# A decoder layer in split single precision: quarter-weight sums and residual operations bound behind given VectorE instructions, at other places, residual tiles in pairs

## The chip, the cores and the metric

One core of one Trainium2 chip runs one program with one launch. The metric is the device time of one execution in microseconds, as the median of several executions. The kernel before takes 1776.06 us (median of 3 executions, 1775.77 to 1781.95).

## The reference, cut to what matters

Sequence of 2048 tokens, width 1024, hidden width 4096, all in float32.

```python
mod = (silu(c) @ w_ada + b_ada)[:, None, :]
sh1, sc1, g1, sh2, sc2, g2 = split(mod, 6)
h = x * (1.0 + sc1) + sh1
gate_b, gate_c, v_conv, v_pool = split(h @ w_in, [512, 1024, 1536])
y_conv = gate_b * short_conv(gate_c * v_conv, conv_w)
y_pool = multiscale_pool(v_pool, w_pool, pool_scale)
mix = concatenate([y_conv, y_pool]) @ w_out
x = layer_norm(ALPHA * x + (1.0 + g1) * mix, ln1_g, ln1_b)
h = x * (1.0 + sc2) + sh2
f = square(relu(h @ w_mlp_in)) @ w_mlp_out
out = layer_norm(ALPHA * x + (1.0 + g2) * f, ln2_g, ln2_b)
```

The change touches two things that this leaves implicit. One is the term `ALPHA * x` of the last line, where x is the first normalisation's output with its scale and shift: the "residual". The other is the weight `w_mlp_out`, of which sums of blocks are formed for a fast product.

## The kernel before, in words

**Split products.** Every matrix product is made of three passes: an operand is cast to a rounded high part on ScalarE (line 84), VectorE subtracts to get the low part (line 85), and TensorE multiplies high by high, high by low and low by high (lines 89 to 91), 128 by 128 weights against 512 columns.

**Seven products in place of eight.** All large products use a Winograd form: of a 2 by 2 partition of both operands, seven block products are formed from sums of blocks, and the results are put together in PSUM banks and by copies and adds. The sums of weight blocks are made by the kernel itself (`sum_blocks`, lines 949 to 960): for each half, four loads by the sync queue, four VectorE operations of 128 by 512, and four stores to DRAM by the GpSimd queue. The operations are all recorded at line 94, the helper `tt`.

**Two blocks of 1024 tokens.** For b = 0 and b = 1 the kernel runs the input projection, the output projection with the first normalisation, the "up" product with relu and square (8 groups of 512 hidden channels, `up`), and the "down" product with the last normalisation (`down`). Up results go to DRAM (`usum`) and are loaded again as operands of down.

**Quarters.** In block 1 three of the seven products of down (FINE) are themselves done by seven products of quarter size (`fine_product`, line 1155 for the matmuls). For these the up groups save quarters of their results (`save_quarters`, `uquart`), and quarter sums of the weights are needed (`quarter_sums`, `wquart`): twelve sums, taken in turn from the list `quarters`. Before the change four of them are written into block 0's down product, at its steps 6, 8, 10 and 12, with tiles "c"; four into block 1's input projection, two each for its groups 1 and 2, with tiles "c"; and four into block 1's up product, after groups 2, 4, 5 and 7 (QUARTER_SUMS), with tiles "o". All are needed before block 1's fine products.

**The residual.** The first normalisation stores its unscaled rows in `nsave`, eight tiles of 128 tokens in each block. Two VectorE operations a tile (`rest_of`, lines 983 and 984) apply the scale and shift rows and ALPHA, and the result is stored in `rsave`, from where the end of down loads it. In block 0 this is done during down (`residual`, two tiles at each of four steps). In block 1 tiles 0 to 3 are done in up groups 1, 3, 5 and 6 (REST): after the second of the seven products the group loads two broadcast rows and the tile (`rest_loads`), and after the fourth `rest_of` is written. Tiles 4 to 7 are done during down (`rest_late`): two at step 0, one at step 2, one at step 4.

**The down product's steps.** Block 0 has 14 steps, each of four operands that are loaded, cast and split one step ahead (`down_operands`); block 1 has 8 and the fine products. Some steps end tile by tile (`by_tile`), so that a finished tile's normalisation can start early (`first_row`, `second_row`, `last`).

**What sets the order.** The text of the kernel gives each instruction's place in a priority order. A planner with a model of durations lays out each engine's stream: an instruction whose inputs and buffers are free in the model may be taken ahead of others that stand before it in the text. On the chip every engine's stream, the queue of transfers on SyncE and that on GpSimd included, is then executed strictly in that order. `tc.issue_after(x)` puts the instructions of its block on x's engine behind x in that order; transfers on other engines are not bound by it. Tiles come from rings by name: "o" has 10 buffers, "c" 2, "r" 5, "w" 6, "h" 28; PSUM has 8 banks. A load into a tile waits until the last user of the buffer is done, a store's landing included.

Of the kernel before, what the change touches and what calls it, by code (L numbers as in the profile page):

```python
# [14 lines left out]
D = 1024  # L15
# [13 lines left out]
HALO = 16  # L29
Q = H // 2  # L30
HALF_SUMS = (1, 2, 3, 3, 3, 3, 3, 0)
QUARTER_SUMS = (0, 0, 1, 0, 1, 1, 0, 1)
EARLY, WARM = 4, 14
WW = T + HALO

# [8 lines left out]
def tile_hybrid_layer(ctx: ExitStack, tc: tile.TileContext, opening, xT, x, wada, vec, win0, win,  # L44
# [20 lines left out]
    def t_o(w=T, dt=F32):  # L65
        return mk(big, [P, w], dt, "o", 10)
# [21 lines left out]
    def mm3(ps, whi, wlo, xhi, xlo, first, last, goes_on=False):  # L88
        nc.tensor.matmul(ps, whi, xhi, start=first, stop=False, skip_group_check=goes_on)  # L89
        nc.tensor.matmul(ps, whi, xlo, start=False, stop=False, skip_group_check=goes_on)  # L90
        nc.tensor.matmul(ps, wlo, xhi, start=False, stop=last, skip_group_check=goes_on)  # L91

    def tt(out_, a, b_, op):
        return nc.vector.tensor_tensor(out_, a, b_, op=op)  # L94


    vecs = cp.tile([P, 104], F32, name="vecs")
# [524 lines left out]
    def in_proj_1(X, W, first_w):  # L622
# [83 lines left out]
        for j in range(1, NG):  # L706
            last = j == NG - 1
            next(groups[j])
            if not last:
                quarter_sums(t_c)  # L710
                next(groups[j])
                quarter_sums(t_c)
            next(groups[j - 1], None)
            if last:
                next(groups[j])
            next(groups[j])
        next(groups[-1], None)
        return ops

# [229 lines left out]
    def sum_blocks(src, dst, tiles=t_o, which=halves):  # L949
        for p in which:  # L950
            a, b_ = tiles(T), tiles(T)
            b22, b12, b11, b21 = a[:, :H], a[:, H:], b_[:, :H], b_[:, H:]
            for i, r in ((3, b22), (1, b12), (0, b11), (2, b21)):
                nc.sync.dma_start(r, src[i][:, p])
            tt(b22, b22, b12, ALU.subtract)
            tt(b12, b12, b11, ALU.subtract)
            tt(b11, b22, b11, ALU.add)
            tt(b21, b21, b11, ALU.subtract)
            for i, r in ((2, b22), (0, b12), (1, b11), (3, b21)):
                nc.gpsimd.dma_start(dst[i][:, p], r)  # L960

    FINE = {0: 2, 1: 0, 5: 1}
    QUARTERED = {1: 0, 7: 1, 0: 2}
    REST = {1: 0, 3: 1, 5: 2, 6: 3}
    UQ = {"11": 0, "12": 1, "22": 2, "s1": 3, "s2": 4, "s3": 5, "s4": 6}

    def save_quarters(r, n, g):
# [18 lines left out]

    quarters = [(n, hf, p) for n in (2, 0, 1) for hf in range(2) for p in halves]

    def quarter_sums(tiles):
        n, hf, p = quarters.pop(0)  # L990
        sum_blocks([w2q[n, i, hf] for i in range(4)], wquart[n, hf], tiles, [p])

    def sum_out(g, tiles):
        sum_blocks([gout[i % 2, i // 2 * 2 + g] for i in range(4)], wosum[g], tiles)
# [1 line left out]
    def up(g, B, fine):  # L996
        X, Y, Z = {}, {}, {}
        order = (0, 1, 5, 4, 6, 7, 3) if g else (0, 1, 7, 4, 5, 6, 3)
        product = seven(summed_weights(w1[g], w1sum[g], order) if g < 2 else block_weights(w1[g]), B)
        ps = [slice(p * H, p * H + H) for p in range(2)]  # L1000

        def keep(banks, tile=t_o):
            r = tile()
            for p in range(2):
                nc.scalar.copy(r[:, ps[p]], banks[p])
            return r

        def add(r, banks):
            for p in range(2):
                tt(r[:, ps[p]], r[:, ps[p]], banks[p], ALU.add)  # L1010

        def join(r, banks):
            add(r, banks)
            nc.scalar.activation(r, r, AF.Relu)
            nc.scalar.activation(r, r, AF.Square)

        def save(r, i):
            if fine and i in QUARTERED and (i or g > 1):
                save_quarters(r, QUARTERED[i], g)
            else:  # L1020
                nc.gpsimd.dma_start(usum[g, i], r)

        def rest_loads():
            if fine and g in REST:
                r, ag, ab = t_o(D), row(t_o(D), rows[0]), row(t_o(D), rows[1])
                nc.sync.dma_start(r, nsave[REST[g]])
                return r, ag, ab

        product(0, X, True)
# [12 lines left out]
        product(2, X, False)  # L1042
        c12 = keep(X)
        if g == 0:
            add(c12, Y)
            join(c12, Z)
            yield
        else:
            product(3, Z, True)
            c22 = keep(Z)  # L1050
        if loaded:
            rest_of(REST[g], *loaded)
        product(4, X, False)
        join(c22, X)
        save(c22, 3)
        if g == 0:
            yield
        else:
            product(5, Z, False)
            join(c12, Z)  # L1060
        s1 = t_o()
        tt(s1, c12, c22, ALU.add)
        tt(c12, c11, c12, ALU.subtract)
        tt(c11, s1, c11, ALU.subtract)
        for i, r in ((4, s1), (6, c12), (5, c11)):
# [53 lines left out]
    def down(b, F, g2, close):  # L1119
# [159 lines left out]
            table[3] = Y, True, third_row  # L1279
        base = 5  # L1280
        by_tile = (3, 4, 6) if b else (4, 5, 6)
        for t in range(8):
            F.append(t_o(D))
        ready = operands(0)
        later = rest_late() if b else residual()
        todo = [(k, m) for k in FINE for m in range(7)]
        for n, (i, hf) in enumerate(steps):
            ops, _ = ready
# [145 lines left out]
    def mlp(b, B, back, g2):  # L1434
# [14 lines left out]
        for g in range(NC):  # L1449
            for _ in ups[g]:  # L1450
                pass
            if b and g in (3, 4):
                c11 = t_o()
                nc.sync.dma_start(c11, usum[g - 3, 0])
                save_quarters(c11, QUARTERED[0], g - 3)
# [79 lines left out]
```

## Time and profile before

| what | value |
|---|---|
| median of 3 executions | 1776.06 us (1775.77 to 1781.95) |
| the profiled execution's own time | 1773.37 us |
| its span, first to last instruction | 1771.6 us |
| TensorE busy, share of the span | 1734.4 us, 98% |
| VectorE busy | 1391.9 us, 79% |
| ScalarE busy | 888.8 us, 50% |
| GpSimd (mostly issuing stores) | 272.0 us, 15% |
| mean granted TensorE clock | 0.989 |
| moved by DMA | 504.64 MB, mean 285 GB/s |

How to read the profile: the page gives one profiled execution. A group row names line, engine, operation, out<-in tiles, shape and count, then busy time and mean duration, then how long the engine was idle just before and what ended that. The timeline gives one instruction a row: start, duration, engine, line, operation, tiles, and in brackets the idle time before it and its releaser. A row of a stretch gives for each engine the busy time and the count, then the granted clock of TensorE, the share of the 16 DMA engines' time, and GB/s. Matmuls of 512 columns follow each other about every 0.23 us, though each is shown as 0.39 us long, because they overlap.

### The profile page before, as it was taken

Reading aid. Unit: us, or ns where it says so; the run is one execution under the profiler, and the core shown is the slowest. Engines: PE = TensorE matmul, PEld = TensorE weight load, DVE = VectorE, ACT = ScalarE, POOL = GpSimd, SP = SyncE. Lnnn points to the kernel's source line nnn. Section 1 sums busy time; section 2 is a strip of 40 time slices with the busy share of each in tenths; the row PEclk is TensorE's granted clock in tenths of the full one; section 3 lists DMA queues with packets and bytes.
Section 4 is the critical chain, followed back from the end, with each engine's and each line's share of the span. In section 5 each row is a group of like instructions: output and inputs, shape, how many; then the busy total and the mean of one; then the engine's idle time right before and its main releaser. Section 6 shows DMA issues by size and latency. Waiting matters only on the chain.

```text
span 1771.6 us, 22926 instructions
## 1 busy us (share of the span) xinstructions
PE 1734.4 (98%) x8142; PEld 1452.7 (82%) x8142; DVE 1391.9 (79%) x1840; ACT 888.8 (50%) x1206; POOL 272.0 (15%) x483
## 2 busy tenths in 40 slices
PE   9999999999999999988999999999999999999998
PEld 8888888888888788866888888878887788999887
DVE  8897788777677776768886789687667677888997
ACT  5323467545444655333673344764444454877451
POOL 0222220123222001111000100103222212000020
PEclk9999999999999999989999999999999999999999
DMA  9999876688887999997872366657677779998871
GB/s 387 344 327 343 301 270 236 263 323 327 325 326 292 344 404 365 353 369 275 282 258 96 107 220 220 215 212 258 214 260 266 263 261 354 418 382 304 294 275 60
DMA packets 157715, 504.64 MB, mean 285 GB/s; under 512 B 18832, under 2 KB 19616, under 8 KB 157600
## 3 DMA queue, kind: packets, MB, share of 16 engines
q1 hardware_dynamic: 108000, 329.61, 51.2%
q0 software_dynamic: 49600, 173.58, 25.6%
q8 instruction: 63, 1.03, 0.2%
q14 instruction: 52, 0.43, 0.1%
HBM read 345.29 MB, written 157.82 MB: 284 GB/s over the span
## 4 chain that ended last, share of the span: by engine, by line
PE 65%; issue 13%; DMA 11%; DVE 8%; POOL 2%; ACT 1%; SPq 0%; DVEq 0%; POOLq 0%; ACTq 0%
PE ps L89 18%; PE ps L90 18%; PE ps L91 18%; PE ps L1155 6%; DVE o L94 3%; PE ps L409 2%; DVE h L85 2%; DMA usum<-c 2%; DMA o<-in_xT 2%; DMA r<-in_w 2%; DVE w L85 1%; DMA c<-in_wada 1%; DMA o<-in_w2q 1%; PE ps L762 1%; DMA r<-uquart 1%
## 5 line engine op out<-in xcount | busy, mean ns | idle before, releaser
L89 PE MATMUL ps<-h,w 128*128 128x512 f32 x1312 | 512.5, 391 | 6.6 <-DVE o L94 6.3
L90 PE MATMUL ps<-h,w 128*128 128x512 f32 x1312 | 512.2, 391 | 1.6 <-DVE h L85 1.6
L91 PE MATMUL ps<-h,w 128*128 128x512 f32 x1312 | 511.8, 390 | 0.4 <-DVE w L85 0.4
L89 PE MATMUL ps<-h,h 128*128 128x512 f32 (+1 forms) x936 | 365.8, 391 | 11.3 <-ACT o L1216 7.3
L90 PE MATMUL ps<-h,h 128*128 128x512 f32 (+1 forms) x936 | 365.9, 391 | 6.0 <-DVE h L85 6.0
L91 PE MATMUL ps<-h,h 128*128 128x512 f32 (+1 forms) x936 | 365.3, 390 | 0.0
L84 ACT CAST h<-r 128x1024 fp32r<-128x1024 f32 (+1 forms) x202 | 205.7, 1022 | 258.7 <-PE ps L90 68.2
L89 PEld LDWEIGHTS ps<-h,w 128*128 128x128 f32 x1312 | 247.2, 189 | 60.4 <-DVE o L94 8.1
L90 PEld LDWEIGHTS ps<-h,w 128*128 128x128 f32 x1312 | 247.2, 188 | 53.3 <-DVE h L85 2.3
L91 PEld LDWEIGHTS ps<-h,w 128*128 128x128 f32 x1312 | 247.3, 188 | 52.7 <-DVE w L85 0.8
L85 DVE TENSOR_TENSOR h<-r,h 128x1024 fp32r<-128x1024 f32 (+1 forms) x202 | 239.0, 1188 | 45.2 <-ACT h L84 44.6
L84 ACT CAST w<-r 128x1024 fp32r<-128x1024 f32 x156 | 164.3, 1054 | 208.8 <-PE ps L90 202.6
L85 DVE TENSOR_TENSOR w<-r,w 128x1024 fp32r<-128x1024 f32 x156 | 190.5, 1221 | 64.4 <-ACT w L84 63.3
L89 PEld LDWEIGHTS ps<-h,h 128*128 128x128 f32 x936 | 177.6, 190 | 49.9 <-ACT o L1216 7.7
L90 PEld LDWEIGHTS ps<-h,h 128*128 128x128 f32 x936 | 177.3, 189 | 43.5 <-DVE h L85 7.6
L91 PEld LDWEIGHTS ps<-h,h 128*128 128x128 f32 x936 | 177.5, 190 | 36.2
L85 DVE TENSOR_TENSOR h<-w,h 128x1024 fp32r<-128x1024 f32 x130 | 160.7, 1236 | 12.7 <-ACT h L84 12.5
L84 ACT CAST h<-w 128x1024 fp32r<-128x1024 f32 x130 | 136.6, 1051 | 9.3 <-DMA w<-in_w 3.4
L94 DVE TENSOR_TENSOR o<-o,o 128x512 f32<-128x512 f32 (+2 forms) x158 | 122.8, 782 | 5.5 <-DMA o<-hsave 2.4
L1155 PE MATMUL ps<-h,h 128*128 128x256 f32 x1008 | 122.9, 285 | 2.1 <-ACT o L1165 2.1
L1155 PEld LDWEIGHTS ps<-h,h 128*128 128x128 f32 x1008 | 122.6, 194 | 2.4 <-ACT o L1165 2.3
L94 DVE TENSOR_TENSOR o<-o,ps 128x512 f32<-128x512 f32 (+1 forms) x150 | 95.8, 650 | 27.8 <-PE ps L91 23.1
(174 smaller groups left out, 1542.9 us busy)
## 6 DMA issues: line engine op xcount, KB each, us to landing
r<-usum SPq DMA_DIRECT2D x88, 512.0 KB, 5.9
w<-w2sum SPq DMA_DIRECT2D x64, 512.0 KB, 6.2
r<-in_w SPq DMA_DIRECT2D x60, 512.0 KB, 6.4
usum<-o POOLq DMA_DIRECT2D x56, 512.0 KB, 4.6
r<-uquart SPq DMA_DIRECT2D x42, 512.0 KB, 8.0
o<-in_w SPq DMA_DIRECT2D x72, 256.0 KB, 5.7
usum<-c POOLq DMA_DIRECT2D x34, 512.0 KB, 5.2
w2sum<-o POOLq DMA_DIRECT2D x64, 256.0 KB, 5.8
```

The source lines that it names most:

```text
L84: high = nc.scalar.copy(hi, src)
L85: return high.ins, nc.vector.tensor_tensor(lo, src, hi.bitcast(F32), op=ALU.subtract).ins
L89: nc.tensor.matmul(ps, whi, xhi, start=first, stop=False, skip_group_check=goes_on)
L90: nc.tensor.matmul(ps, whi, xlo, start=False, stop=False, skip_group_check=goes_on)
L91: nc.tensor.matmul(ps, wlo, xhi, start=False, stop=last, skip_group_check=goes_on)
L94: return nc.vector.tensor_tensor(out_, a, b_, op=op)
L409: nc.tensor.matmul(ps[m, h], wt[:, w : w + P], A[k][p // 2][:, hs], start=k == 0 and p == 0, stop=k == KD - 1 and p == 2)
L762: nc.tensor.transpose(ps[:, t * P : t * P + P], R[4 * h + t][:, k * P : k * P + P], ident)
L1155: nc.tensor.matmul(ps, a[:, us], w[:, gs], start=not begun, stop=hf == 1 and g == 3 and a is ul, skip_group_check=True)
```

## The change

The four edits:

1. `tt` remembers its last instruction in `recent`. `quarter_sums` takes an instruction, and its VectorE operations are bound behind that.
2. The places of the twelve quarter sums: five in block 0's down product (steps 2, 3, 6, 7, 10, each behind the last split of the next step's operands), four in block 1's input projection (behind the last `tt` at two places of groups 1 and 2, the second place now at the end of the turn), three in block 1's up product (after groups 1, 3 and 5). The tiles of the gate vector's loads (`ada` at steps 0 and 1) come from "o" in place of "c". The quarters of groups 0 and 1 that are loaded again (`save_quarters`) are bound too, after groups 3 and 5 in place of 3 and 4.
3. Block 1's residual tiles 0 to 5 are done in pairs in up groups 2, 4 and 6. Two rows and two tiles are loaded at the same place as before, and the operations are written at the end of the group, bound behind its last `tt`.
4. Residual tiles 6 and 7 are both done at step 0 of block 1's down product, bound behind the last split of the next step's operands. Their rows come from "o" tiles that are taken before the eight result tiles.

```diff
-QUARTER_SUMS = (0, 0, 1, 0, 1, 1, 0, 1)
+QUARTER_SUMS = (0, 1, 0, 1, 0, 1, 0, 0)
...
+    recent = [None]
+
     def tt(out_, a, b_, op):
-        return nc.vector.tensor_tensor(out_, a, b_, op=op)
+        done = nc.vector.tensor_tensor(out_, a, b_, op=op)
+        recent[0] = done.ins
+        return done
...
             if not last:
-                quarter_sums(t_c)
+                quarter_sums(t_c, recent[0])
                 next(groups[j])
-                quarter_sums(t_c)
             next(groups[j - 1], None)
             if last:
                 next(groups[j])
             next(groups[j])
+            if not last:
+                quarter_sums(t_c, recent[0])
...
-    REST = {1: 0, 3: 1, 5: 2, 6: 3}
+    REST = {2: (0, 1), 4: (2, 3), 6: (4, 5)}
...
-    def quarter_sums(tiles):
+    def quarter_sums(tiles, after):
         n, hf, p = quarters.pop(0)
-        sum_blocks([w2q[n, i, hf] for i in range(4)], wquart[n, hf], tiles, [p])
+        with tc.issue_after(after):
+            sum_blocks([w2q[n, i, hf] for i in range(4)], wquart[n, hf], tiles, [p])
...
             if fine and g in REST:
-                r, ag, ab = t_o(D), row(t_o(D), rows[0]), row(t_o(D), rows[1])
-                nc.sync.dma_start(r, nsave[REST[g]])
-                return r, ag, ab
+                loaded = [row(t_o(D), rows[0]), row(t_o(D), rows[1])]
+                for t in REST[g]:
+                    loaded.append(t_o(D))
+                    nc.sync.dma_start(loaded[-1], nsave[t])
+                return loaded
...
-        if loaded:
-            rest_of(REST[g], *loaded)
         product(4, X, False)
...
         save(c11, 7)
+        if loaded:
+            with tc.issue_after(recent[0]):
+                for t, r in zip(REST[g], loaded[2:]):
+                    rest_of(t, r, *loaded[:2])
...
     def rest_late():
-        ag, ab = row(t_c(D), rows[0]), row(t_c(D), rows[1])
-        for t in range(4, 8):
-            yield
+        ag, ab = row(t_o(D), rows[0]), row(t_o(D), rows[1])
+        for t in range(6, 8):
+            after = yield
             r = t_r()
             nc.sync.dma_start(r, nsave[t])
-            rest_of(t, r, ag, ab)
+            with tc.issue_after(after[1]):
+                rest_of(t, r, ag, ab)
...
             if b == 0 and n < 2:
-                ada(G2 + 4 * n, G2 + 4 * n + 4, nc.sync.dma_start, lambda: t_c(D))
-            if b == 0 and n in (6, 8, 10, 12):
-                quarter_sums(lambda w: t_c(w))
+                ada(G2 + 4 * n, G2 + 4 * n + 4, nc.sync.dma_start, lambda: t_o(D))
+            if b == 0 and n in (2, 3, 6, 7, 10):
+                quarter_sums(t_c, ready[1][1])
...
-            if n == (0 if b else base):
+            if b and n == 0:
+                later.send(ready[1])
...
-            for _ in range({0: 2, 2: 1, 4: 1}.get(n, 0) if b else 0):
-                next(later, None)
...
-            if b and g in (3, 4):
+            if b and g in (3, 5):
...
-                quarter_sums(t_o)
+                quarter_sums(t_o, recent[0])
```

More of the change, by code (lines that the diff above doesn't have):

```diff
@@ L1281, in down @@
         by_tile = (3, 4, 6) if b else (4, 5, 6)
+        if b:
+            later = rest_late()
+            next(later)
+        else:
+            later = residual()
         for t in range(8):
@@ L1284, in down @@
         ready = operands(0)
-        later = rest_late() if b else residual()
         todo = [(k, m) for k in FINE for m in range(7)]
@@ L1293, in down @@
             if b == 0 and n < 2:
-                ada(G2 + 4 * n, G2 + 4 * n + 4, nc.sync.dma_start, lambda: t_c(D))
-            if b == 0 and n in (6, 8, 10, 12):
-                quarter_sums(lambda w: t_c(w))
+                ada(G2 + 4 * n, G2 + 4 * n + 4, nc.sync.dma_start, lambda: t_o(D))
+            if b == 0 and n in (2, 3, 6, 7, 10):
+                quarter_sums(t_c, ready[1][1])
             if b == 0 and 2 <= n < 6:
                 sum_x(n - 2, ready[1])
-            if n == (0 if b else base):
+            if b and n == 0:
+                later.send(ready[1])
+                try:
+                    later.send(ready[1])
+                except StopIteration:
+                    pass
+            if b == 0 and n == base:
                 next(later)
-            for _ in range({0: 2, 2: 1, 4: 1}.get(n, 0) if b else 0):
-                next(later, None)
             if b == 0 and base <= n < base + 4:
@@ L1451, in mlp @@
                 pass
-            if b and g in (3, 4):
+            if b and g in (3, 5):
                 c11 = t_o()
-                nc.sync.dma_start(c11, usum[g - 3, 0])
-                save_quarters(c11, QUARTERED[0], g - 3)
+                nc.sync.dma_start(c11, usum[g // 2 - 1, 0])
+                with tc.issue_after(recent[0]):
+                    save_quarters(c11, QUARTERED[0], g // 2 - 1)
             for _ in range(QUARTER_SUMS[g] if b else 0):
-                quarter_sums(t_o)
+                quarter_sums(t_o, recent[0])
             for make, src, dst, p in sums[:HALF_SUMS[g]]:
```

## The prediction

> **What bounds the kernel now.** I read the page's first table, then TensorE's waits, then the trace cut into stretches around each wait, and last the VectorE, ScalarE and SyncE rows in those stretches.
>
> ```profile
> span 1771.6 us, 22926 instructions
> PE 1734.4 (98%) x8142; PEld 1452.7 (82%) x8142; DVE 1391.9 (79%) x1840; ACT 888.8 (50%) x1206; POOL 272.0 (15%) x483
> ...
> PE ps L90 <- DVE h L85: 7.6, 5, 3.6
> PE ps L89 <- DVE o L94: 7.3, 4, 3.6
> PE ps L89 <- ACT o L1216: 7.3, 1, 7.3
> PE ps L1155 <- ACT o L1165: 2.1, 1, 2.1
> ```
>
> TensorE is the bound: 1734.4 of 1771.6 us. No matmul is touched by the change, so it can only win back waits, or add some. The rows say which of the others is late: a split (L85), an add that empties a PSUM bank (L94), a copy that does so (L1216, L1165). Each wait costs more than its own length, as the stretches show (columns: length; busy and count of PE, PEld, DVE, ACT, POOL; granted clock; DMA share; GB/s):
>
> ```profile
> 754.00:768.00 14.00, 6.69 (x20) 4.99 (x19) 7.49 (x8) 5.93 (x8) 2.17 (x4) 0.63 1.00 374
> 825.00:850.00 25.00, 18.21 (x56) 13.48 (x57) 25.00 (x39) 19.59 (x33) 1.62 (x3) 0.80 0.80 272
> 893.00:1045.00 152.00, 152.00 (x672) 125.92 (x671) 119.30 (x146) 70.38 (x107) 10.87 (x17) 1.00 0.43 149
> 1171.00:1194.00 23.00, 20.08 (x86) 15.30 (x84) 22.85 (x24) 16.50 (x19) 0.53 (x1) 1.00 0.35 129
> 1194.00:1371.00 177.00, 177.00 (x782) 146.34 (x781) 126.26 (x168) 84.04 (x101) 48.42 (x77) 1.00 0.68 248
> 1371.00:1379.00 8.00, 6.07 (x20) 4.54 (x19) 7.36 (x8) 1.82 (x2) 0.54 (x1) 0.79 0.57 231
> 1412.00:1424.00 12.00, 8.40 (x27) 6.41 (x26) 10.98 (x12) 3.39 (x4) 1.08 (x2) 0.72 0.24 100
> 1517.00:1526.00 9.00, 6.91 (x46) 6.71 (x45) 8.81 (x10) 8.03 (x10) 0.00 (x0) 0.81 1.02 416
> ...
> 1550.00:1600.00 50.00, 50.00 (x419) 50.00 (x418) 42.26 (x44) 36.46 (x48) 0.00 (x0) 1.00 0.98 375
> ```
>
> In the undisturbed row of 177 us, 782 matmuls take 0.226 us each; in the fine products (last row) 0.119. What a stretch lost is its length less its matmuls at that price. 754 to 768: 14 - 20 x 0.226 = 9.5 us. 825 to 850: 25 - 56 x 0.226 = 12.3. 1171 to 1194: 23 - 86 x 0.226 = 3.6. 1371 to 1379: 8 - 20 x 0.226 = 3.5. 1412 to 1424: 12 - 27 x 0.226 = 5.9. 1517 to 1526: 9 - 46 x 0.119 = 3.5. Together 38.3 us. That is more than the waits alone, because the granted clock falls after most of them (0.63, 0.80, 0.79, 0.72, 0.81). The Trainium skill, TensorE: Matmul & The Clock Gate (Part 1: The HAM clock gate), puts the half clock behind an idle window of about 3.4 us; the 1371 stretch disagrees, since its one wait (row below) was 1.93 us and the clock still fell to 0.79. By the page that stretch would have lost only 1.9 us, and the term below would be 1.6 us smaller.
>
> **Part 1: the first six residual tiles of block 1.** Before, one tile each in groups 1, 3, 5 and 6 of the up product, its two VectorE operations placed wherever the planner put them; now two each in groups 2, 4 and 6, behind the group's last subtraction.
>
> ```profile
> 1369.24 1.23 DVE L983 SCALAR_TENSOR_TENSOR o<-o,o 128x1024 f32<-128x1024 f32 x1 [5.06 <-DMA o<-nsave]
> 1372.78 0.68 DVE L94 TENSOR_TENSOR o<-o,ps 128x512 f32<-128x512 f32 x1
> 1412.95 1.23 DVE L983 SCALAR_TENSOR_TENSOR o<-o,o 128x1024 f32<-128x1024 f32 x1 [10.46 <-DMA o<-nsave]
> 1373.52 0.50 PE L89 MATMUL ps<-h,w 128*128 128x512 f32 x1 [1.93 <-DVE o L94]
> 1417.10 0.79 PE L89 MATMUL ps<-h,w 128*128 128x512 f32 x1 [3.60 <-DVE o L94]
> ...
> DMA to landing us min/median/max: 9.5/12.2/13.2
> ```
>
> Here VectorE stood 5.06 and 10.46 us in front of L983, whose tile was still on its way (the last row is L1026's own: 9.5 to 13.2 us), while the add that frees TensorE's banks was queued behind it; TensorE waited 1.93 and 3.60 us for that add. In the new place the load is still issued after the second product, and five products of 24 matmuls lie between: 5 x 24 x 0.226 = 27 us, twice the slowest landing. So both stalls go: 3.5 + 5.9 = **9.4 us** gained. The price is a burst at the group's end: four operations of 1.23 us, 4.9 us, ahead of the next group's splits and sums. In the 177 us row VectorE is idle for 51 us, so I take nothing for it; uncovered it is up to 4.9 us in three groups, 14.7, against the 9.4. Either way the two broadcast rows are now loaded for three groups, not four.
>
> The same edit takes the operations out of group 1, which is interleaved with the end of the output projection:
>
> ```profile
> 1164.85 1.23 DVE L983 SCALAR_TENSOR_TENSOR o<-o,o 128x1024 f32<-128x1024 f32 x1 [2.15 <-DMA o<-nsave]
> ```
>
> In the stretch from 1171 VectorE is busy 22.85 of 23 us, so TensorE waits for VectorE's work itself. Gone ahead of it are the wait of 2.15 and two operations, 2.15 + 2 x 1.23 = 4.6 us, more than the 3.6 lost. I take **3 us** (0 to 3.6).
>
> **Part 2: quarter sums.** Twelve sums, each four loads, four operations and four stores, feed the fine products of block 1. Before, four were written into block 0's down product, four into block 1's input projection, four into the up product. What the trace shows is another thing:
>
> ```profile
> L960 POOL DMA_DIRECT2D wquart<-c x32: 542/543/548, 688.7 to 854.7; - x32
> L94 DVE TENSOR_TENSOR c<-c 128x512 f32<-128x512 f32 x16 | 11.0, 690 | 25.3 <-DMA c<-in_w2q 25.0
> ...
> 794.07 0.69 DVE L94 TENSOR_TENSOR c<-c 128x512 f32<-128x512 f32 x1 [8.23 <-DMA c<-in_w2q]
> 806.36 0.69 DVE L94 TENSOR_TENSOR c<-c 128x512 f32<-128x512 f32 x1 [4.88 <-DMA c<-in_w2q]
> 809.15 0.68 DVE L94 TENSOR_TENSOR o<-o,ps 128x512 f32<-128x512 f32 x1
> 812.72 0.73 ACT L741 ACTIVATE tmp<-o,mv 128x512 f32<-128x512 f32 x1 [24.07 <-DVE mv L739]
> 825.96 0.51 PE L89 MATMUL ps<-h,h 128*128 128x512 f32 x1 [1.63 <-ACT h L84]
> ```
>
> All 32 stores of the eight sums on "c" tiles are issued between 688.7 and 854.7, inside the down product: the four written into the input projection were pulled up into it. And VectorE stood 25.0 us idle for their loads. The worst of it: step 9 of the down product ends by tile, and its first finished row is ready when tile 0 is, but VectorE waited 8.23 and 4.88 us for sums first and came to it at 809.15; ScalarE, in order, stood 24.07 us for its statistics with the casts of the next operands queued behind; at 825.96 TensorE ran out. That is the stretch that lost 12.3 us, with VectorE busy for all its 25.
>
> Now five sums stay in the down product (steps 2, 3, 6, 7, 10), each bound behind the last split of the next step's operands, four go into the input projection behind its adds, three into the up product. In the steps that feed this stretch only that of step 10 remains, its load issued as soon as the sum of step 7 lets its tiles go. Of the 13.1 us of waits ahead of 809.15 little is left, and about 13 us is what the stretch lacked. I take **10 us** (0 to 12.3).
>
> The four sums that now do run in the input projection cost 4 x 4 x 0.69 = 11 us of VectorE, which is idle there for 152 - 119.3 = 32.7 us, with the DMA at 0.43: nothing. Uncovered it is 11 us.
>
> The stall at 754 has another cause:
>
> ```profile
> 745.09 1.23 DVE L94 TENSOR_TENSOR r<-r,o 128x1024 f32<-128x1024 f32 x1 [9.16 <-DMA r<-nsave]
> 761.20 1.55 ACT L1216 COPY o<-ps 128x512 f32<-128x512 f32 x3
> 761.83 0.79 PE L89 MATMUL ps<-h,h 128*128 128x512 f32 x1 [7.31 <-ACT o L1216]
> ```
>
> VectorE stands 9.16 us for a residual tile, the splits behind it come late, "r" buffers come free late, and the copy that frees the bank stands behind casts on ScalarE. Block 0's residual operations are not touched. The sums of steps 6 and 7 fall just ahead of this wait and into the stall: 2.8 us each. Nothing of 9.5 or all of it could go, or a sum's 2.8 us be added; I take **2 us** gained, nearer to the untouched wait.
>
> **Part 3: the front of the fine products.** The sum after the last up group is gone (the last stores are now those of group 5), and the residual tiles 6 and 7 take the place of 4 and 5 at step 0, bound behind a split, with their rows in "o" tiles.
>
> ```profile
> L960 POOL DMA_DIRECT2D wquart<-o x16: 542/555/583, 1276.1 to 1498.4; - x16
> 1497.77 1.05 ACT L84 CAST h<-r 128x1024 fp32r<-128x1024 f32 x1 [12.77 <-DMA r<-uquart]
> ```
>
> ScalarE waited 12.77 us for a load while that sum's loads and stores were in the queues, and the 1517 stretch, whose copy is late, lost 3.5. With 2 MB and 2.8 us of VectorE less ahead of it I take **2 us** (0 to 3.5). Tiles 6 and 7 also leave the last stage; TensorE is not short there, so nothing.
>
> **New waits.** Two sums now run at steps 2 and 3, where the queues are already full:
>
> ```profile
> 623.00:644.00 21.00, 21.00 (x94) 17.42 (x93) 13.73 (x16) 12.67 (x15) 0.00 (x0) 1.00 1.02 413
> 644.00:666.00 22.00, 22.00 (x98) 18.22 (x98) 16.95 (x18) 11.67 (x12) 2.13 (x4) 1.00 1.03 419
> ```
>
> Eight transfers of 0.26 MB a sum are 2.1 MB; two are 4.2 MB, at 0.416 MB/us 10 us of transfer that the operands stand behind. TensorE has no wait there and operands are prepared ahead, so part of it is hidden; for this, for the up groups' bursts and for the conditioning tiles that now share "o" buffers I take one new stall the size of the 1371 one, **3.5 us** lost (0 to 14.7). The Trainium skill, DMA: Bandwidth & Descriptors (Specifications), gives an HBM limit of about 358 GB/s a core; by it the 4.2 MB would take 11.7 us. These rows, at 413 and 419, show more.
>
> **The sum.** 9.4 + 3 + 10 + 2 + 2 - 3.5 = 22.9 us. The profiled execution took 1773.4 us, so 1750.5; the median of the runs is 2.7 us above that execution, so **1753 us**, 1.3% faster.
>
> **Rivals.** (a) Only the residual's edit pays: the down product stays as short of VectorE and buffers as before, since the finished rows and the residual's own waits remain. For it: the 9.16 us wait is untouched. Against: 13.1 us of waits for sums lie right ahead of the stall. Then 9.4 + 3 - 2 = 10.4: 1766. (b) Steps 2 and 3 run dry: the 10 us come out at TensorE. For it: DMA 1.02 and 1.03. Against: no wait there now. 22.9 - 10 + 3.5 = 16.4 less: 1760. (c) Slower: "o" buffers. The pair and its two rows now hold four of ten "o" tiles from the second product to the group's end, where three were held for a shorter time, and the copies that empty the banks need one.
>
> ```profile
> 1363.69 0.59 ACT L1005 COPY o<-ps 128x512 f32<-128x512 f32 x1 [5.33 <-DMA uquart<-o]
> ```
>
> Here a bank's copy already stood 5.33 us until a store let an "o" tile go. If the four held tiles bring this to two copies in each of groups 2 to 6, 10 x 5.33 = 53 us of ScalarE wait; it decides once it outlasts a spare product of 5.4 us, and if two thirds reach TensorE, 35 - 22.9: 12 us slower, 1788. Against: quarter sums (two tiles) now fall in odd groups and pairs in even ones. (d) The binding changes nothing, because the planner had these orders anyway: 1776. Against: the 32 stores by 854.7.
>
> **How the numbers follow.** A measurement can tell about 0.5%, 9 us, from no change. Forecast 0.60, (a) 0.17, (b) 0.10, (c) 0.08, (d) 0.05. Faster by over 0.5% (below 1767) holds the forecast, (b) and a little under half of (a): 0.76; the rest of (a) and (d) are 0.16 the same; (c) is 0.08. All upper terms and no new stall give 38 us, 1738; (a) with the split stall grown by 2.8 us gives 1769. The range is 1740 to 1771.
>
> **What would show it.** Right: no TensorE wait near L983 in the up groups; stores of "c" sums spread to about 1000 us; no VectorE wait for w2q loads in front of the finished rows, and the 825 stretch at full clock. Half right: the L1216 wait of 7 us still there. Wrong: bank copies waiting for "o" tiles in groups 2 to 6, TensorE waiting at 630 to 690, or the 12 us stall in its old place.

## The result, and the profile after

The kernel after takes 1755.24 us (median of 4 executions, 1752.75 to 1759.73); before, measured beside it, takes 1778.24 (1775.77 to 1781.95). The ratio is 0.9872, with a 95% interval of 0.9841 to 0.9902: 1.3% faster. The profiled executions are 1756.75 and 1773.37 us, 16.6 apart, where the medians are 23.0 apart: the one of before is 4.9 us under its median here, the one of after 1.5 over its own. The trace therefore has 16.6 us to explain.

Of after, the page's line of the engines:

```profile
PE 1725.4 (98%) x8142; PEld 1448.3 (83%) x8142; DVE 1390.0 (79%) x1840; ACT 887.3 (51%) x1206; POOL 270.3 (15%) x483
```

The same 8142 matmuls, and VectorE has the same work. What TensorE waited for (total, times, longest, in us), of after:

```profile
PE ps L89 <- ACT o L1011: 13.9, 4, 5.2
PE ps L91 <- DVE w L85: 3.7, 1, 3.7
```

and two waits of before that lie outside the stretches of the prediction:

```profile
580.22 0.50 PE L90 MATMUL ps<-h,h 128*128 128x512 f32 x1 [0.76 <-DVE h L85]
1723.79 0.50 PE L89 MATMUL ps<-h,h 128*128 128x512 f32 x1 [1.02 <-DVE o L94]
```

The split (h L85), the bank copy of the down product (L1216) and the add behind the residual (o L94), 22.2 us together before, are nearly gone. The first place is taken by a wait that before did not have: 13.9 us for L1011, the copy of the up product that empties a bank (L1005 before). The stretches of after, with the columns of the prediction's table (length; busy and count of PE, PEld, DVE, ACT, POOL; clock; DMA; GB/s):

```profile
600.00:710.00 110.00, 110.00 (x487) 91.00 (x486) 85.08 (x97) 59.92 (x64) 10.74 (x20) 1.00 1.00 395
754.00:768.00 14.00, 14.00 (x63) 11.59 (x63) 5.60 (x6) 4.68 (x6) 0.54 (x1) 1.00 1.01 376
798.00:825.00 27.00, 27.00 (x121) 22.36 (x120) 27.00 (x42) 19.50 (x33) 3.24 (x6) 1.00 0.82 280
1010.00:1020.00 10.00, 6.85 (x23) 5.49 (x24) 8.40 (x10) 1.53 (x2) 2.73 (x4) 0.83 0.69 239
1166.00:1172.00 6.00, 4.84 (x21) 3.48 (x20) 6.00 (x8) 4.37 (x5) 0.00 (x0) 1.00 0.11 43
1262.00:1268.00 6.00, 3.85 (x17) 2.93 (x16) 3.98 (x7) 4.83 (x8) 2.05 (x3) 1.00 0.94 298
1315.00:1319.00 4.00, 3.45 (x15) 2.53 (x15) 3.54 (x4) 1.65 (x2) 0.00 (x0) 1.00 0.02 5
1341.00:1353.00 12.00, 6.98 (x22) 5.29 (x22) 9.19 (x12) 5.82 (x8) 3.14 (x5) 0.72 0.77 267
1386.00:1391.00 5.00, 3.55 (x16) 2.62 (x15) 0.81 (x2) 1.55 (x3) 1.32 (x3) 1.00 1.03 415
1427.00:1439.00 12.00, 6.75 (x22) 5.10 (x21) 9.10 (x12) 5.82 (x8) 3.14 (x5) 0.72 0.85 287
1500.00:1510.00 10.00, 10.00 (x85) 10.00 (x85) 9.65 (x10) 8.53 (x10) 0.00 (x0) 1.00 1.02 417
```

Both places of the down product run through at full clock (the one that lost 12.3 us before now comes at 798 to 825, with VectorE just as busy and no wait), and so does the front of the fine products (1500 to 1510). At 0.226 us a matmul the others lost: 4.8 us at 1010, 1.3 at 1166, 2.2 at 1262, 0.6 at 1315, 7.0 at 1341, 1.4 at 1386, 7.0 at 1427. Together 24.3 us, against the 38.3 of before: 14.0 of the 16.6. Of the other 2.6, 2.5 are three waits of before outside the prediction's table that after does not have: the two rows above, 0.76 and 1.02 us, and one of 0.72 at 579.

**The new wait.** Of after, VectorE, ScalarE and TensorE around the stretch at 1341 (start, duration):

```profile
1337.48 0.68 DVE L96 TENSOR_TENSOR c<-c,ps 128x512 f32<-128x512 f32 x1
...
1338.42 2.35 DVE L988 SCALAR_TENSOR_TENSOR o<-o,o 128x1024 f32<-128x1024 f32 x2
1340.69 2.35 DVE L989 SCALAR_TENSOR_TENSOR o<-o,o 128x1024 f32<-128x1024 f32 x2
1342.96 0.68 DVE L96 TENSOR_TENSOR c<-c,ps 128x512 f32<-128x512 f32 x1
1343.67 1.06 ACT L1020 ACTIVATE c<-c 128x1024 f32<-128x1024 f32 x1 [11.57 <-DVE c L96]
1346.53 1.54 ACT L1011 COPY o<-ps 128x512 f32<-128x512 f32 x3
1347.14 0.80 PE L89 MATMUL ps<-h,w 128*128 128x512 f32 x1 [5.02 <-ACT o L1011]
```

The two `c<-c,ps` adds are the `join` of the next group's second product. The four residual operations stand between them, 1338.42 to 1342.96, so the second add comes 5.5 us after the first. The relu (L1020) needs both; ScalarE is in order, and the bank copy L1011 is behind the relu; TensorE waits 5.02 us for the bank. Before, the same two adds:

```profile
1352.65 0.68 DVE L94 TENSOR_TENSOR c<-c,ps 128x512 f32<-128x512 f32 x1
...
1353.59 0.68 DVE L94 TENSOR_TENSOR c<-c,ps 128x512 f32<-128x512 f32 x1
```

0.94 us apart. `issue_after` says what the operations come behind, not what comes behind them: they are bound to the last subtraction of group 4 but stand in the middle of group 5's adds. The stretch at 1427 (after group 6) shows the same order, and the one at 1262 (after group 2) a milder case.

### The profile page after: what moved, and what is told of

The parts are those of the page before. It is cut to its first block, busy times and chain, and to the rows that moved or that the text cites. A ratio compares the mean times of both kernels' runs of the same rounds, so it can differ in the third digit from the quotient of the medians.

```text
span 1755.0 us, 22936 instructions
## 1 busy us (share of the span) xinstructions
PE 1725.4 (98%) x8142; PEld 1448.3 (83%) x8142; DVE 1390.0 (79%) x1840; ACT 887.3 (51%) x1206; POOL 270.3 (15%) x483
## 4 chain that ended last, share of the span: by engine, by line
PE 84%; DMA 6%; issue 4%; DVE 4%; ACT 1%; POOL 0%; SPq 0%; DVEq 0%; POOLq 0%; ACTq 0%
PE ps L89 25%; PE ps L90 25%; PE ps L91 25%; PE ps L1166 7%; PE ps L413 3%; DMA r<-in_w 2%; DMA usum<-c 2%; DVE o L96 1%; PE ps L767 1%; DMA o<-hsave 1%; DMA o<-in_w2q 1%; DVE w L85 1%; POOL usum L1027 0%; DVE o L988 0%; DVE c L96 0%
## 5 line engine op out<-in xcount | busy, mean ns | idle before, releaser
L89 PE MATMUL ps<-h,w 128*128 128x512 f32 x1312 | 513.2, 392 | 15.6 <-ACT o L1011 13.9
L85 DVE TENSOR_TENSOR h<-r,h 128x1024 fp32r<-128x1024 f32 (+1 forms) x202 | 238.5, 1185 | 63.6 <-ACT h L84 63.3
L85 DVE TENSOR_TENSOR w<-r,w 128x1024 fp32r<-128x1024 f32 x156 | 190.4, 1221 | 69.5 <-ACT w L84 68.8
L91 PEld LDWEIGHTS ps<-h,h 128*128 128x128 f32 x936 | 175.8, 188 | 36.0
L89 PEld LDWEIGHTS ps<-h,h 128*128 128x128 f32 x936 | 175.8, 188 | 35.9
L90 PEld LDWEIGHTS ps<-h,h 128*128 128x128 f32 x936 | 175.8, 188 | 35.5
L85 DVE TENSOR_TENSOR h<-w,h 128x1024 fp32r<-128x1024 f32 x130 | 159.5, 1227 | 8.1 <-ACT h L84 7.9
L1166 PEld LDWEIGHTS ps<-h,h 128*128 128x128 f32 x1008 | 121.1, 192 | 0.1
```

The lines of the kernel that those rows point to most:

```text
L85: return high.ins, nc.vector.tensor_tensor(lo, src, hi.bitcast(F32), op=ALU.subtract).ins
L1166: nc.tensor.matmul(ps, a[:, us], w[:, gs], start=not begun, stop=hf == 1 and g == 3 and a is ul, skip_group_check=True)
```

## The experiments

The first theory: the gain is the binding alone (a sum that is not bound is taken before its load has landed, and VectorE stands), the places do little, and the burst between two adds gives part back. The rivals: the places make the gain, or the residual's edit does. Four kernels on one chip, before at 1776.26 us beside them.

**The residual's edit alone.** The sums, the quarters that are loaded again and the tiles of the gate vector's loads as before, in their old places and unbound (the main lines against after):

```diff
-QUARTER_SUMS = (0, 1, 0, 1, 0, 1, 0, 0)
+QUARTER_SUMS = (0, 0, 1, 0, 1, 1, 0, 1)
...
-        with tc.issue_after(after):
+        with nullcontext():
...
-            if b == 0 and n in (2, 3, 6, 7, 10):
+            if b == 0 and n in (6, 8, 10, 12):
```

> The residual's edits alone (pairs in up groups 2, 4 and 6 behind the group's last operation, tiles 6 and 7 at step 0); the quarter sums stay at their old places and free. Theory: in the up product the pairs lose about what they win (the two stalls of 9.4 us behind L983 go, three new ones of 2.2, 7.0 and 7.0 us come), the group 1 stretch wins 2 to 3 us, and the down product of block 0 keeps its two stalls (9.5 and 12.3 us): 1771 to 1780, within 0.4% of before. Rival: the pairs' new stalls come from the sums' new places beside them (shared "o" buffers); then this kernel has none of them and is 12 us faster than before, about 1766.

1773.38 us, ratio 0.9983 (0.9966 to 1.0001): nothing that can be told from no change. Its copies of the up product already make TensorE wait 8.3 us.

**The sums alone.** The residual's operations and loads as in before, the rest as in after (the one line that stands for it):

```diff
-    REST = {2: (0, 1), 4: (2, 3), 6: (4, 5)}
+    REST = {1: 0, 3: 1, 5: 2, 6: 3}
```

> The quarter sums' edits alone (binding and new places, and the gate vector's loads in "o" tiles); the residual as before. Theory: the down product's two stalls go (21.8 us), the input projection gains one of 4.8 us, the stalls of 3.5 and 5.9 us behind L983 stay and the new ones of the pairs are absent: 15 to 20 us faster than before, 1757 to 1763. Rival: the residual's edits carry half of the gain, as the forecast's 9.4 and 3 had it; then 8 to 10 us faster, 1768 to 1770.

1746.67 us (1743.55 to 1748.83), ratio 0.9829 (0.9799 to 0.9858): some 10 us faster than expected, and 8.6 faster than after. The two intervals overlap, but no execution of the one comes into the range of the other. Its waits of TensorE:

```profile
PE ps L89 <- DVE o L96: 4.4, 3, 2.9
PE ps L91 <- DVE w L85: 4.1, 2, 3.7
```

No wait for L1011. Of the two stalls behind unbound residual operations one is left, 2.9 us; the other has gone though the operations were not touched. The up product, first of this kernel, then of after:

```profile
1260.00:1440.00 180.00, 177.01 (x771) 145.38 (x770) 126.32 (x164) 85.16 (x103) 44.52 (x71) 0.99 0.72 260
```

```profile
1260.00:1440.00 180.00, 165.55 (x706) 134.58 (x705) 126.85 (x167) 80.36 (x97) 46.36 (x75) 0.96 0.69 250
```

In the same 180 us, 771 matmuls against 706. So the residual's edit costs on top of the sums'.

**Bound, in the old places; and free, in the new ones.** Both against after; in the first the input projection's second sum of a turn is in its old place too:

```diff
-QUARTER_SUMS = (0, 1, 0, 1, 0, 1, 0, 0)
+QUARTER_SUMS = (0, 1, 0, 1, 0, 1, 0, 1)
...
-            if b == 0 and n in (2, 3, 6, 7, 10):
+            if b == 0 and n in (6, 8, 10, 12):
```

> The changed kernel with binding kept, but the sums of block 0's down product at the old steps 6, 8, 10 and 12, those of the input projection at the old places, and the twelfth after up group 7. Theory that binding is what counts (sums of the input projection no longer pulled into the down product): both down stalls stay away, the fine products' front stall of about 3.5 us may return: 1752 to 1762. Rival that the places count (earlier steps clear of the finished rows): sums of steps 10 and 12 stand again among the rows of steps 9 to 11 and 5 to 22 us come back: 1760 to 1777.

1759.40 us, ratio 0.9901 (0.9875 to 0.9927). And:

```diff
     def quarter_sums(tiles, after):
...
-        with tc.issue_after(after):
+        with nullcontext():
```

> The changed kernel with the sums at their new places, but free: their operations are not bound. Theory that binding is what counts: the sums written into the input projection are pulled into the down product again, their last stores lie before 880 us, and the two stalls (21.8 us) come back in most part: 1768 to 1778. Rival that the places count: 1752 to 1760, with both stretches at full clock.

1774.10 us, ratio 0.9988 (0.9976 to 1.0001). With the residual's edit in all four kernels:

| | old places | new places |
|---|---|---|
| sums free | 1773.38 | 1774.10 |
| sums bound | 1759.40 | 1755.24 (after) |

Binding is worth 14.0 us in the old places and 18.9 in the new, and the intervals of the ratios do not meet; the places are worth -0.7 and 4.2, where they do. (After was measured beside a before of 1778.24 us, the other three beside 1776.26; by the ratios the binding is worth 0.8% and 1.2%.) Only in the new places do the two kernels differ by the sums' binding alone; in the old places the free one also has the old tiles for the gate vector and the old, unbound reload of quarters. The down product shows why. What VectorE waited for between 676 and 860 us: before; after; free in old places; bound in old places; free in new places:

```profile
DVE c L94 <- DMA c<-in_w2q: 26.4, 8, 8.2
DVE r L94 <- DMA r<-nsave: 18.6, 4, 9.2
```

```profile
DVE r L96 <- DMA r<-nsave: 24.7, 4, 8.3
```

```profile
DVE c L96 <- DMA c<-in_w2q: 30.7, 9, 10.8
DVE r L96 <- DMA r<-nsave: 17.7, 4, 8.5
```

```profile
DVE r L96 <- DMA r<-nsave: 20.5, 4, 9.6
```

```profile
DVE c L96 <- DMA c<-in_w2q: 25.7, 7, 7.2
DVE r L96 <- DMA r<-nsave: 18.0, 3, 9.2
```

In this stretch the waits for the sums' loads (in_w2q) are there in every free kernel and in no bound one; the residual's (nsave) are in all five. And TensorE's stretches, free in old places, free in new places, bound in old places:

```profile
754.00:774.00 20.00, 12.00 (x41) 9.36 (x40) 12.92 (x14) 8.46 (x11) 2.75 (x6) 0.74 1.02 380
825.00:856.00 31.00, 21.27 (x70) 15.32 (x69) 31.00 (x48) 23.41 (x40) 2.15 (x4) 0.83 0.82 279
```

```profile
750.00:764.00 14.00, 9.28 (x36) 7.25 (x35) 4.84 (x6) 5.91 (x9) 0.00 (x0) 0.88 0.93 332
815.00:850.00 35.00, 23.83 (x80) 17.29 (x79) 35.00 (x54) 24.13 (x43) 3.79 (x7) 0.80 0.87 301
```

```profile
754.00:768.00 14.00, 14.00 (x64) 11.58 (x63) 10.91 (x10) 5.25 (x6) 1.07 (x2) 1.00 0.85 300
825.00:850.00 25.00, 25.00 (x112) 20.69 (x111) 18.38 (x26) 9.73 (x10) 0.00 (x0) 1.00 0.81 291
```

Both stalls come back when the sums are free, wherever they are written (10.7 and 15.2 us lost, 5.9 and 16.9), and neither is there when they are bound.

Binding does two things at once that these kernels do not part. Unbound, eight or nine sums run inside the down product (their stores on "c" tiles all come by 859.0 and 855.3 us); bound, four or five do. So it could be the number of sums there that costs, and not VectorE's waits for their loads. Against that stands a kernel below, with six bound sums in the down product and no wait of TensorE in it; eight bound sums were not tried. Nor are waits for loads enough by themselves: bound in the old places, VectorE still stands 12.4 us for sums' loads in the input projection, and the only wait of TensorE behind them is 3.60 us, where after has one of 3.73.

**Away with the burst.** If the four operations between two adds cost 16 us, other places for them should give that back. Three kernels tried, before at 1777.14 beside the first two. One tile behind the adds of the fifth product and one behind those of the sixth:

```diff
         join(c22, X)
+        if loaded:
+            with tc.issue_after(recent[0]):
+                rest_of(REST[g][0], loaded[2], *loaded[:2])
...
             join(c12, Z)
+            if loaded:
+                with tc.issue_after(recent[0]):
+                    rest_of(REST[g][1], loaded[3], *loaded[:2])
...
         save(c11, 7)
-        if loaded:
-            with tc.issue_after(recent[0]):
-                for t, r in zip(REST[g], loaded[2:]):
-                    rest_of(t, r, *loaded[:2])
```

> The changed kernel, but each pair's operations are taken apart: one tile's two operations behind the last add of the fifth product, the other's behind the last add of the sixth, where both banks have been emptied. Theory that the pairs' new stalls come from four operations standing between the two adds of the next group's second product: TensorE's waits for the copy at L1011 (13.9 us in the changed kernel, 17.6 us with the half clock) go to under 4 us and the kernel takes 1738 to 1745. Rival that the four held "o" tiles starve that copy: the waits stay above 8 us and the time at 1748 to 1755.

1748.07 us, ratio 0.9842 (0.9821 to 0.9862), with these waits:

```profile
PE ps L91 <- DVE w L85: 7.5, 3, 3.7
PE ps L89 <- ACT o L1011: 4.4, 2, 3.3
```

L1011 falls from 13.9 to 4.4 us, close to what the theory has, and 3.3 of the 4.4 stand behind a copy that itself stood 6.75 us for an "o" tile. By the medians 7.2 us of the time come back, less than expected (the intervals of the ratios overlap, the times of single executions do not). For TensorE now waits for splits of weights, 7.5 us in place of 3.7: the operations stand among the splits there. Another place, the pair behind the adds of the next group's second product:

```diff
+    held = []
...
         join(c11, Y)
+        if held:
+            with tc.issue_after(recent[0]):
+                while held:
+                    rest_of(*held.pop(0))
...
-            with tc.issue_after(recent[0]):
-                for t, r in zip(REST[g], loaded[2:]):
-                    rest_of(t, r, *loaded[:2])
+            held.extend((t, r, *loaded[:2]) for t, r in zip(REST[g], loaded[2:]))
```

> The changed kernel, but each pair's four operations stand behind the last add of the next group's second product, so that the burst keeps its size and the four "o" tiles are held longer. Theory of the burst between the adds: with both adds ahead of it most of the 17.6 us goes, some of it coming back where the burst now delays the splits behind it: 1740 to 1748. Rival of the "o" tiles: held longer, they starve the copies more: 1758 to 1770.

1755.27 us, ratio 0.9878 (0.9859 to 0.9897): no gain, so the time is what neither side expected. The bank copies' wait halves to 7.1 us, and 6.7 of these are another thing, the rival's: two copies that themselves stood 5.45 and 5.49 us for an "o" tile. Of the waits behind the adds 0.35 us is left. At splits stand 7.9 us, of which 3.7 are the wait in the input projection that after has too, and 4.2 come behind the burst. Third, one tile a group, so that the burst is two operations, before at 1777.52:

```diff
-    REST = {2: (0, 1), 4: (2, 3), 6: (4, 5)}
+    REST = {1: (0,), 2: (1,), 3: (2,), 4: (3,), 5: (4,), 6: (5,)}
```

> The changed kernel, but one residual tile in each of up groups 1 to 6, still behind the group's last operation: the burst is halved (two operations, about 2.3 us) and comes six times; three "o" tiles are held in each group. Theory of the burst: what is left of each stall is the burst less the slack, about 4.6 - 2.3 us below the 5.2 us seen, so single waits of at most 2.9 us at L1011 and in sum under 9 us, with less half clock: 1742 to 1751. Rival that the place between the two adds costs the same whatever the size: six waits of about 5 us, 1768 to 1780.

1749.68 us, ratio 0.9844 (0.9822 to 0.9865), a time as expected. Its VectorE at the place of 1341:

```profile
1338.80 0.68 DVE L96 TENSOR_TENSOR c<-c,ps 128x512 f32<-128x512 f32 x1
...
1339.73 1.22 DVE L988 SCALAR_TENSOR_TENSOR o<-o,o 128x1024 f32<-128x1024 f32 x1
1340.87 0.68 DVE L96 TENSOR_TENSOR c<-c,ps 128x512 f32<-128x512 f32 x1
1341.47 1.22 DVE L989 SCALAR_TENSOR_TENSOR o<-o,o 128x1024 f32<-128x1024 f32 x1
```

The order is not quite that of after with half the burst: only the first of the two operations stands between the adds, the second behind them, and so it is in all six groups. The adds are 2.1 us apart, and in none of the six does a wait of TensorE for a bank copy come from them. So four operations between the adds cost and one does not, at the same place; two between them were not seen. The waits that are left at L1011, 4.7 and 2.1 us, belong to copies that stood for an "o" tile; the 4.7 is more than the 2.9 that was expected of a single wait.

**The input projection's wait.** The last of its four sums moved to step 12 of the down product:

```diff
-            if not last:
+            if j == 1:
                 quarter_sums(t_c, recent[0])
...
-            if b == 0 and n in (2, 3, 6, 7, 10):
+            if b == 0 and n in (2, 3, 6, 7, 10, 12):
```

> The changed kernel, but the second sum of the input projection's group 2 is written into step 12 of block 0's down product, bound like the others. Theory that this sum's operations, standing between the sums of the fourth group's weights, make the split late for which TensorE waits at 1013 us (3.7 us, 4.8 us with the half clock): the wait goes and the kernel takes 1749 to 1752. Rival that the fourth group's own work makes it: the wait stays within 1 us of 3.7, and the time at 1754 to 1757.

```profile
1010.00:1020.00 10.00, 10.00 (x45) 8.27 (x45) 10.00 (x12) 5.58 (x7) 2.59 (x4) 1.00 0.64 218
```

The stretch that lost 4.8 us loses none, so that sum made the wait. But the time is 1755.67 us, ratio 0.9877 (0.9854 to 0.99), no gain: the wait after group 2, 2.15 us in after, became 4.04 us, and 1.1 us of waits came at 906. Both moves together:

> The edits of the two kernels before last together (a tile's operations behind the adds of the fifth and the sixth product; the last sum of the input projection at step 12). If both theories hold and their gains add: 1755 - 16 - 5 = 1734, within 1731 to 1741, clear of the kernel with the sums' edits alone. If the waits only move elsewhere: 1745 to 1755.

1744.70 us (1744.42 to 1745.39), ratio 0.9822 (0.9804 to 0.9839): the fastest, though short of what was expected, with 8.0 us of waits for splits left.

**The "o" buffers.** In the kernel with one tile a group the remaining waits for L1011 (6.7 us) are copies that stood for an "o" tile. An eleventh "o" buffer, with the room taken from a small ring:

```diff
-        return mk(big, [P, w], dt, "o", 10)
+        return mk(big, [P, w], dt, "o", 11)
...
-        wr = mk(sm, [P, P], F32, "wp", 6)
+        wr = mk(sm, [P, P], F32, "wp", 4)
...
-    REST = {2: (0, 1), 4: (2, 3), 6: (4, 5)}
+    REST = {1: (0,), 2: (1,), 3: (2,), 4: (3,), 5: (4,), 6: (5,)}
```

> The kernel with the half bursts and one buffer more in the ring "o" (11 in place of 10; the ring "wp" of the folded weights in block 0 has 4 in place of 6 to make room). Theory that its two remaining waits for the copy at L1011 (4.7 and 2.1 us of TensorE, 11.2 us of ScalarE behind stores of uquart) are waits for an "o" buffer: they go or fall under 2 us in sum, and the kernel is 5 to 10 us faster than with ten buffers, 1740 to 1746. Rival that the copy waits for its stores whatever the buffers (the stores themselves are late): both waits stay, 1747 to 1752.

What ScalarE waited for with ten buffers, and with eleven:

```profile
ACT o L1011 <- DMA uquart<-o: 11.2, 2, 5.8
```

```profile
ACT o L1011 <- DMA uquart<-o: 3.1, 1, 3.1
```

No wait of TensorE for L1011 is left: the cause of these two waits is shown. The time hardly moves and misses what was expected, 1748.70 us, ratio 0.9849 (0.9829 to 0.9869), before at 1776.19; in place of the 6.7 us stand 7.1 for the adds `o<-o,ps` behind weight loads (in_w) that landed late.

**The faster base.** From the sums alone: the single residual tiles bound behind the fifth product's adds, and then, in the second kernel, the last sum of the input projection moved as well.

```diff
-        if loaded:
-            rest_of(REST[g], *loaded)
         product(4, X, False)
         join(c22, X)
+        if loaded:
+            with tc.issue_after(recent[0]):
+                rest_of(REST[g], *loaded)
```

> The sums' edits with the residual at its old groups (1, 3, 5 and 6, one tile each), but each tile's two operations bound behind the last add of the fifth product. Theory: the wait at L983 for its load (2.9 us of TensorE in group 6, 4.6 with the half clock) goes, and a burst of two operations behind the adds costs under 2 us: 1741 to 1746. Rival that VectorE's work in the up product is short of slack wherever two operations more are placed: 1746 to 1752.

> The kernel before this one in the list, with the last sum of the input projection at step 12 of the down product as well. Theory that the two edits are independent: the wait at 1013 us (4.8 us with the half clock) goes too, 1736 to 1742. Rival, as in the earlier kernel where that edit gained nothing in sum: 1741 to 1747.

1749.38 us, ratio 0.9842 (0.9827 to 0.9856), and 1746.24, ratio 0.9821 (0.9804 to 0.9838): neither better than the sums alone, and both in the range of the rival. Of the first:

```profile
1396.58 1.22 DVE L96 TENSOR_TENSOR r<-r,r 128x1024 f32<-128x1024 f32 x1 [8.30 <-DMA r<-in_w]
1397.73 0.68 DVE L96 TENSOR_TENSOR o<-o,ps 128x512 f32<-128x512 f32 x1
1398.46 0.79 PE L89 MATMUL ps<-h,w 128*128 128x512 f32 x1 [6.59 <-DVE o L96]
```

The residual is no longer ahead of the add; a sum of weight blocks is, whose load came 8.30 us late.

## Why the prediction came out, step by step

The time, 1753 forecast and 1755.24 measured, came out through errors in both directions, so that it lies so close is luck: 26.4 us of gains and 3.5 of loss were forecast. In the traces the steps below gained 37.0 (9.4 + 2.3 + 12.3 + 9.5 + 3.5), new waits took 23.0, and the 2.6 outside the table make it 16.6.

- **Stalls behind L983, +9.4.** Right: both are gone. But the sums alone removed one of them too, so only part belongs to the binding of the residual.
- **The burst, taken at 0.** This step failed: "In the 177 us row VectorE is idle for 51 us, so I take nothing for it". It cost 2.2 + 7.0 + 7.0 = 16.2 us, more than the "uncovered" bound of 14.7. The idle time was spread over 177 us; the burst stood between two adds 0.94 us apart, with ScalarE's relu and bank copies behind them. Each 7.0 is a wait of 5.0 or 5.3 us and about 2 us lost to the lower clock after it (0.72). That this order was the cause is shown by the kernels that took the operations away from between the adds: the waits behind the adds went. With it the residual's edit in the up groups is a loss, 9.4 - 16.2 = -6.8, which the kernel with the sums alone agrees with.
- **Group 1, +3.** 3.6 before, 1.3 after: 2.3.
- **The sums in the down product, +10.** 12.3, as far as the signs go by the named mechanism: no VectorE wait for w2q loads in the down product, and "c" stores spread out:

```profile
L965 POOL DMA_DIRECT2D wquart<-c x36: 540/542/552, 632.1 to 998.8; - x36
```

  to 998.8 us, where before had all by 854.7. But it is the binding that does it; the emphasis on steps 2, 3, 6, 7 and 10 was wrong, as the old places bound show.
- **The stall at 754, +2 of 9.5.** This step failed: "The stall at 754 has another cause". The wait for nsave that was named is still there (8.3 us its longest, 24.7 in total, more than before) and TensorE does not notice. The stall went with the binding of the sums. That VectorE's waits for their loads, 10.1 us between 687 and 718 in before, had used up the slack ahead of it is the likely way, but not shown apart. A wait on the chain of the stall was taken for its cause, when by itself it does not make the stall.
- **The front of the fine products, +2.** 3.5, all of it.
- **The input projection, 0.** Failed: "VectorE, which is idle there for 152 - 119.3 = 32.7 us ... nothing". It lost 4.8 us, a bound sum among the splits; the same mistake as with the burst.
- **New waits, -3.5.** 16.2 + 4.8 + 0.6 + 1.4 = 23.0.

The rivals. (a), only the residual's edit pays: refuted, it is the other way round. (b), steps 2 and 3 run dry: the stretch of 600 to 710 has DMA at 1.00 and 395 GB/s, and TensorE runs all 110 us. (c), the "o" buffers: the mechanism exists and is at work, but it cost after only 1.4 us, at 1386, for a copy that had stood 5.38 us for an "o" tile; the forecast price of 35 us was far off. (d), the binding changes nothing: refuted by both pairs of the table. In the chances, 0.76 holds a third of (a), not "a little under half"; nothing else hangs on it.

**What stays open.** Each later move removed the wait it aimed at and gave back less than that wait: 9.5 us off L1011 gave 7.2, the 3.7 at the split gave nothing, 6.7 off the "o" tiles nothing that can be told (ratios 0.9844 and 0.9849). In each case other waits came up: late splits in the up groups in the first, a longer wait for the bank copy after group 2 in the second, late weight loads in the third. Pairs with eleven "o" buffers were not tried, nor two operations between the adds. Why those loads land late in one order and not in another (the issue order on the sync queue, or the moment when "r" tiles come free) was not tried apart. The sums alone, both moves together, and the last kernel (1746.67, 1744.70, 1746.24) can't be told from each other.

## What to carry to other kernels

On an engine that executes in order, work that was hoisted ahead of its own load's landing blocks everything behind it: bind it behind work that is due anyway, and look first at where that engine stands waiting for loads, not at how much it does. Before a burst is called hidden, look at the two instructions that it will stand between and at who waits for the second one: idle time averaged over a stretch says nothing about that place. And a wait that stands in front of a stall is a cause only if the stall goes with it; test that before leaving the stall in the sum.

## What the runs showed of the hardware

The loss of clock after a wait does not follow from the wait's length. In the kernel with both moves, two waits of TensorE for the same line:

```profile
1330.04 0.50 PE L91 MATMUL ps<-h,w 128*128 128x512 f32 x1 [2.91 <-DVE w L85]
1410.59 0.67 PE L91 MATMUL ps<-h,w 128*128 128x512 f32 x1 [2.94 <-DVE w L85]
```

and their stretches:

```profile
1327.00:1334.00 7.00, 4.09 (x18) 3.30 (x18) 7.00 (x12) 1.04 (x2) 3.12 (x5) 1.00 0.95 320
1408.00:1415.00 7.00, 4.41 (x12) 3.50 (x13) 7.00 (x11) 0.00 (x0) 2.69 (x5) 0.76 0.96 341
```

2.91 us left the clock at 1.00, 2.94 took it to 0.76, and six matmuls more were lost: behind the second wait the next matmuls start about 0.43 us apart (1411.06, 1411.48, 1411.91 and on) in place of 0.23. In the kernel with eleven buffers the longer of two waits is the one that cost nothing: 2.95 us at 1321 left the clock at 1.00, 2.80 us at 1401 took it to 0.81 (the stretches 1317 to 1324 and 1397 to 1406). In before a wait of 1.93 us was enough (0.79, in the prediction); in after one of 2.15 at 1264 was not (the stretch at 1262, 1.00). So the price of a wait of 2 to 3 us is not to be read from its length alone. The Trainium skill, TensorE: Matmul & The Clock Gate (Part 1: The HAM clock gate), puts the half clock behind an idle window of about 3.4 us; the waits of 1.93 and 2.94 us, which halved it too, disagree with that figure. The same part says that the window runs freely; that two waits of one length end differently fits this, and no run here tried it apart.
